# Moving the load buffers of a streaming matrix-vector kernel to a multiple of 4096 bytes in SBUF

## The chip, the cores and the metric

The kernel runs on one core of a Trainium2 chip. The metric is the device time of one execution in microseconds (us), as a median of several.

## The reference, cut to what matters

```python
def setup_inputs():
    B, S, D = 8, 2048, 4096
    # x: (B, S, D) float32, 268 MB;  w: (D, 1) float32

def reference(x, w):
    proj = (x @ w).squeeze(-1)
    cm = np.maximum.accumulate(proj, axis=1)
    is_record = (proj >= cm).astype(np.float32)
    return np.cumsum(is_record, axis=1).astype(np.float32)
```

Every number of `x` is used once. What costs is to bring 268 MB into the core.

## The kernel before

Three buffers of 64 KB in each of the 128 partitions are filled in turn. VectorE (DVE) multiplies the first 2816 columns of every row by `w` and adds them up; GpSimd (POOL) multiplies the other 1280, and ScalarE (ACT) adds those up. The names matter here because the tiles of a pool lie in SBUF in the order in which they are made:

```python
    W2, W2C = 1248, 544
    # ... cut ...
    identity = sb([P, P], "identity")
    small = sb([P, 352], "small")
    masked = sb([P, 2 * P], "masked")
    fold = sb([P, 2 * B - H + Q], "fold")
    w2 = sb([P, W2C], "w2")
    xall = sb([P, NS * R * D], "xall")
    xbuf = [xall[:, i * R * D : (i + 1) * R * D] for i in range(NS)]
    w_sb = sb([P, PC], "w_sb")
    cm = sb([B, N], "cm")
    cnt = sb([B, N], "cnt")
```

The loads of the main part, and the two engines' work on a load:

```python
        for g in range(NG):          # RS = (4, 4, 4, 3) rows for each partition
            r = RS[g]
            for t in range(B):
                i = SY.dma_start(
                    out=at(g, t)[:, : r * D],
                    in_=x[B - 1 - t, STARTS[g] : STARTS[g] + r * P, :].rearrange(
                        "(p r) d -> p (r d)", r=r
                    ),
                ).then_inc(xs[t], 16)
                u, n = user_before(g, t)
                if n:
                    i._wait_ge(*(free(u, n)))     # the buffer's last use
    # ... cut ...
                    i = dot(xb[:, j * D : j * D + VC], w_v[:, :VC], ...)      # DVE
    # ... cut ...
                    i = G.tensor_mul(out=xl, in0=xl, in1=w_sb).then_inc(pl, 1)  # POOL
```

So a packet of a load is the whole run of one partition: 65536 bytes in 24 loads, 49152 in eight. The last 128 rows of each sequence come as 16384-byte rows (six loads), and the last two of those tiles in seven pieces by columns, so that little work is left when the last byte lands:

```python
    LAST = [
        (B - 2, 1696, D, (1696, VC), (VC, D)),      # columns; DVE's; POOL's
        (B - 2, 0, 1696, (0, 1696), None),
        (B - 1, 2592, D, (2592, CV), (CV, D)),
        (B - 1, 1440, 2592, (1792, 2592), (1440, 1792)),
        (B - 1, 736, 1440, (736, 1248), (1248, 1440)),
        (B - 1, 352, 736, (352, 736), None),
        (B - 1, 0, 352, (0, 352), None),
    ]
```

`w2` holds the weights that POOL needs for two of these pieces.

## Time and profile before

| | before |
|---|---|
| median time | 631.98 us (three runs, 631.68 to 632.14) |
| profiled span | 630.0 us |
| bytes read | 268.45 MB |
| address of the load buffers in a partition | 21952 = 85 x 256 + 192 |

From the page of the kernel before: the span, the busy time of each engine, then the share of time in which the DMA engines were busy and what they moved, in 40 equal slices of the span, then the packets.

```profile
span 630.0 us, 1182 instructions
...
PE 31.7 (5%) x108; PEld 15.1 (2%) x108; DVE 406.9 (65%) x292; ACT 180.4 (29%) x273; POOL 370.1 (59%) x147
...
DMA  9999999999999999999999999999999999999995
GB/s 400 399 466 399 466 408 458 421 442 433 433 441 424 445 424 441 425 445 420 449 416 454 412 458 408 458 408 458 408 425 437 444 418 437 444 415 440 416 424 230
DMA packets 6579, 268.55 MB, mean 426 GB/s; under 512 B 768, under 2 KB 1040, under 8 KB 1584
```

The DMA engines are at 90% or more in every slice but the last, while the busiest engine, DVE, works 65% of the span. The GB/s of single slices swing and are not to be read one by one; means over longer stretches are steadier. From the view of stages of before (start and end in us, length, busy time of the engines, granted clock, DMA share, GB/s), a stretch of one load, one of the middle, and one of the 49152-byte packets:

```profile
23.00:42.30 19.30, 0.00 (x0) 0.00 (x0) 12.12 (x8) 5.45 (x8) 11.50 (x4) 1.00 1.00 435
160.00:460.00 300.00, 7.14 (x32) 4.08 (x32) 197.60 (x133) 85.87 (x126) 182.01 (x64) 0.79 1.00 434
460.00:580.00 120.00, 3.29 (x16) 1.94 (x16) 81.01 (x55) 32.81 (x49) 70.42 (x26) 0.51 1.00 432
```

In the stretch of one load (19.3 us) DVE has 12.1 us of work and POOL 11.5, so both wait for the next load. The waits of before (engine and tile that waited, for whom, us in total, times, longest):

```profile
POOL xall L287 <- POOLq L290: 250.2, 32, 20.9
DVE xall L127 <- DMA xall<-in_x_dram: 187.8, 32, 7.9
```

DVE waits for each of the 32 big loads; POOL is started by DVE's signal, so its 250.2 us are the same waits at second hand. The chain of waits of before, in order of time (start, us, what), says so too:

```profile
22.98 0.03 POOLq L290
...
333.61 0.03 POOLq L290
...
345.14 7.81 issue
352.95 0.03 POOLq L290
352.99 11.50 POOL xall L287 x4
364.48 7.83 issue
```

The chain goes through POOL, but every 11.5 us of it is followed by 7.8 us of "issue", time in which POOL waits for something that the view does not name: the landing of the next load, passed on by DVE. What repeats every 19.34 us (352.95 - 333.61) is the load. At the end of the kernel, from the timeline of before (start, us, engine, line, operation):

```profile
623.09 0.99 DVE L127 CUSTOM_DVE_ANT_0 xall<-xall,w_v 128x800 f32<-128x800 f32 x1 [0.26 <-DMA xall<-in_x_dram]
...
624.00 0.68 DVE L127 CUSTOM_DVE_ANT_0 xall<-xall,w_v 128x512 f32<-128x512 f32 x1
...
624.61 0.55 DVE L127 CUSTOM_DVE_ANT_0 xall<-xall,w_v 128x384 f32<-128x384 f32 x1
...
625.09 0.52 DVE L127 CUSTOM_DVE_ANT_0 xall<-xall,w_v 128x352 f32<-128x352 f32 x1
...
627.11 0.34 DVE L149 TENSOR_TENSOR_SCAN cnt_l<-ps,cnt_l,small 8x64 f32<-8x64 f32 x1
```

From 623.09 us on DVE waits for no load any more: its last four pieces run back to back, and a short chain of DVE and two matmuls ends the kernel. One of the four pieces is the one that the change makes wider.

### The profile page before, as it was taken

The numbers are of one execution on the slowest core, as the hardware profiler recorded it, in microseconds if no ns is written. First come the engines' busy times: TensorE is split into PE (matmuls) and PEld (weight loads), VectorE is DVE, ScalarE is ACT, GpSimd is POOL, SyncE is SP. The second block draws the span as 40 slices with busy tenths as digits, with TensorE's granted clock in tenths as the row PEclk, the third lists the DMA queues.
The fourth block names the chain that finished last, engine by engine and source line by source line (L and its number), as shares of the span: only waits on it lengthen the run. The fifth ranks groups of instructions, "written<-read, shape, count | busy, mean of one in ns | idle before, by whom it ended". The sixth has DMA issues, their size and how long they took to land.

```text
span 630.0 us, 1182 instructions
## 1 busy us (share of the span) xinstructions
PE 31.7 (5%) x108; PEld 15.1 (2%) x108; DVE 406.9 (65%) x292; ACT 180.4 (29%) x273; POOL 370.1 (59%) x147
## 2 busy tenths in 40 slices
PE   8000000000010000000010000000002000000031
PEld 3000000000010000000010000000001000000010
DVE  0755676546785557755579555676557966655897
ACT  1222332123322233222233222332223232232353
POOL 0555676446765557755567555576555766666685
PEclk9999999999999999999996555555555555555555
DMA  9999999999999999999999999999999999999995
GB/s 400 399 466 399 466 408 458 421 442 433 433 441 424 445 424 441 425 445 420 449 416 454 412 458 408 458 408 458 408 425 437 444 418 437 444 415 440 416 424 230
DMA packets 6579, 268.55 MB, mean 426 GB/s; under 512 B 768, under 2 KB 1040, under 8 KB 1584
## 3 DMA queue, kind: packets, MB, share of 16 engines
q1 hardware_dynamic: 6560, 268.50, 98.8%
q10 hardware_dynamic: 16, 0.02, 0.0%
q14 instruction: 3, 0.02, 0.0%
HBM read 268.45 MB, written 0.07 MB: 426 GB/s over the span
## 4 chain that ended last, share of the span: by engine, by line
POOL 52%; issue 38%; DMA 6%; PE 2%; DVE 1%; SPq 0%; POOLq 0%; ACT 0%; ACTq 0%
POOL xall L287 52%; DMA xall<-in_x_dram 6%; PE w_v L231 2%; PE ps L231 0%; DVE xall L127 0%; SPq L199 0%; DMA w<-in_w_dram 0%; POOLq L290 0%; ACT w L242 0%; PE ps L373 0%; DVE cm_l L143 0%; DVE cnt_l L149 0%; DVE ps L146 0%; ACT xall L133 0%; DVE masked L365 0%
## 5 line engine op out<-in xcount | busy, mean ns | idle before, releaser
L127 DVE CUSTOM_DVE_ANT_0 xall<-xall,w_v 128x2816 f32<-128x2816 f32 (+3 forms) x133 | 388.4, 2974 | 187.8 <-DMA xall<-in_x_dram 187.8
L287 POOL TENSOR_TENSOR xall<-xall,w_sb 128x1280 f32<-128x1280 f32 x120 | 344.9, 2909 | 250.2 <-POOLq L290 250.2
L133 ACT ACTIVATE xall<-xall 128x1280 f32<-128x1280 f32 (+1 forms) x130 | 162.8, 1252 | 429.7 <-POOL xall L287 417.1
L319 PE MATMUL ps<-identity,small 128*8 128x128 f32 x60 | 13.1, 410 | 572.0 <-PEq L316 572.0
L133 ACT ACTIVATION_READ_ACCUMULATOR xall<-xall 128x1 f32 x130 | 24.2, 186 | 0.0
L343 POOL TENSOR_TENSOR xall<-xall,w_sb 128x1280 f32<-128x1280 f32 (+1 forms) x8 | 21.6, 2704 | 2.8 <-DMA xall<-in_x_dram 2.8
L319 PEld LDWEIGHTS ps<-identity,small 128*8 128x8 f32 x60 | 7.5, 128 | 578.8 <-issue 574.8
L143 DVE TENSOR_TENSOR_SCAN cm<-ps,cm,small 8x512 f32<-8x512 f32 (+1 forms) x5 | 6.1, 1216 | 14.1 <-PE ps L319 14.1
L231 PE MATMUL w_v<-w,identity 8*128 8x512 f32 x14 | 12.1, 1056 | 0.0
L127 DVE DVE_READ_ACCUMULATOR2_ANT small<- 128x1 f32 x133 | 10.8, 82 | 0.0
L253 DVE MEMSET ps<- 8x512 f32 x1 | 0.5, 485 | 15.5 <-ACT w L242 15.5
L149 DVE TENSOR_TENSOR_SCAN cnt<-ps,cnt,small 8x512 f32<-8x512 f32 (+1 forms) x5 | 6.1, 1217 | 0.2
L373 PE MATMUL ps<-fold,masked 128*8 128x64 f32 x32 | 4.6, 303 | 20.1 <-ACT masked L361 13.2
L231 PEld LDWEIGHTS w_v<-w,identity 8*128 8x128 f32 x14 | 4.6, 332 | 7.3 <-issue 7.3
L239 ACT COPY w_sb<-w_v 128x768 f32<-128x768 f32 x1 | 0.8, 799 | 11.4 <-PE w_v L231 11.4
L146 DVE TENSOR_TENSOR ps<-ps,cm 8x512 f32<-8x512 f32 (+1 forms) x5 | 3.3, 660 | 0.2
L373 PEld LDWEIGHTS ps<-fold,masked 128*8 128x8 f32 x32 | 2.5, 112 | 22.4 <-ACT masked L361 14.6
L361 ACT ACTIVATE masked<-fold,small 128x8 f32<-128x8 f32 x9 | 2.5, 297 | 0.2
L231 PE MATMUL ps<-w,identity 8*128 8x512 f32 x2 | 2.1, 1136 | 2.6 <-DMA w<-in_w_dram 2.6
L238 ACT ACT_TABLE_LOAD x1 | 1.3, 1283 | 2.7 <-DVE fold L249 2.7
L245 DVE TENSOR_REDUCE fold<-identity 128x2 f32<-128x128 f32 x1 | 0.3, 286 | 2.1 <-POOL cnt L224 2.1
L343 POOL TENSOR_TENSOR xall<-xall,w 128x352 f32<-128x352 f32 (+1 forms) x2 | 1.5, 766 | 0.2 <-DMA xall<-in_x_dram 0.2
(23 smaller groups left out, 7.0 us busy)
## 6 DMA issues: line engine op xcount, KB each, us to landing
xall<-in_x_dram SPq DMA_DIRECT2D x8, 6144.0 KB, 30.5
xall<-in_x_dram SPq DMA_DIRECT2D x6, 2048.0 KB, 39.5
xall<-in_x_dram SPq DMA_DIRECT2D x1, 1200.0 KB, 33.5
xall<-in_x_dram SPq DMA_DIRECT2D x1, 848.0 KB, 35.1
xall<-in_x_dram SPq DMA_DIRECT2D x1, 752.0 KB, 36.3
xall<-in_x_dram SPq DMA_DIRECT2D x1, 576.0 KB, 37.1
xall<-in_x_dram SPq DMA_DIRECT2D x24, 45.0
xall<-in_x_dram SPq DMA_DIRECT2D x1, 352.0 KB, 17.4
```

What stands on the lines that cost most here:

```text
L127: return V.tensor_tensor_reduce(out=xsl, in0=xsl, in1=wsl, scale=1.0, scalar=0.0, op0=ALU.mult, op1=ALU.add, accum_out=dst,)
L133: return A.activation(out=xsl, in_=xsl, func=ACTF.Copy, accum_out=dst)
L143: V.tensor_tensor_scan(out=cm_, data0=src, data1=low, initial=cm0, op0=ALU.max, op1=ALU.max,)._wait_ge(psr, base).then_inc(psr, 1)
L146: V.tensor_tensor(out=src, in0=src, in1=cm_, op=ALU.is_ge)._wait_ge(psr, base + 1).then_inc(psr, 1)
L149: V.tensor_tensor_scan(out=cnt_, data0=src, data1=low, initial=cnt0, op0=ALU.add, op1=ALU.max,)._wait_ge(psr, base + 2).then_inc(cs, 1)
L231: i = T.matmul(out=dst, lhsT=identity[:NW, k : k + 1].to_broadcast([NW, P]), rhs=w_row, start=True, stop=True,).then_inc(bw, 1)
L238: A.copy(out=w_sb[:, CV - VC :], in_=ps)._wait_ge(bw, 1).then_inc(wc, 1)
L287: i = G.tensor_mul(out=xl, in0=xl, in1=w_sb).then_inc(pl, 1)
L319: i = T.matmul(out=ps[:B, j : r * P : r], lhsT=l[:, j * B : (j + 1) * B], rhs=identity, start=k == 0, stop=k == 1,)
L343: G.tensor_mul(out=xl, in0=xl, in1=w_pool(*p))._wait_ge(xq[i], 16).then_inc(pl, 1)
L361: A.activation(out=e, in_=on, func=ACTF.Copy, scale=acc)._wait_ge(*wait).then_inc(ms, 1)
L373: return T.matmul(out=ps[:B, q : q + Q], lhsT=e, rhs=by_i, start=start, stop=bool(stop),)._wait_ge(*((mg, on_g) if pool else (ms, on_a)))
```

## The change

The intent is to let every load be written to an aligned place. Two small tables move behind the buffers. To make the rest in front of them end on a multiple of 4096, the weights' table `w2` shrinks from 544 to 512 columns (`WC` is 512), and for that one POOL piece gives 32 columns to DVE. No instruction is added or removed.

```diff
-        (B - 1, 736, 1440, (736, 1248), (1248, 1440)),
+        (B - 1, 736, 1440, (736, 1280), (1280, 1440)),
...
-    W2, W2C = 1248, 544
+    W2, W2C = 1280, WC
...
     identity = sb([P, P], "identity")
     small = sb([P, 352], "small")
-    masked = sb([P, 2 * P], "masked")
-    fold = sb([P, 2 * B - H + Q], "fold")
     w2 = sb([P, W2C], "w2")
     xall = sb([P, NS * R * D], "xall")
     xbuf = [xall[:, i * R * D : (i + 1) * R * D] for i in range(NS)]
     w_sb = sb([P, PC], "w_sb")
     cm = sb([B, N], "cm")
     cnt = sb([B, N], "cnt")
+    masked = sb([P, 2 * P], "masked")
+    fold = sb([P, 2 * B - H + Q], "fold")
```

In the built program the buffers' address goes from 21952 to 20480. Each of the three is 65536 bytes long, so all of them have the same remainder.

## The prediction

> **What bounds the kernel now.** The load stream. The slices of the page show the DMA engines at 90% or more in every slice but the last, 426 GB/s over the span; DVE is busy 65%, POOL 59%. In the view of stages, the stretch 23.0 to 42.3 us has DMA share 1.00 at 435 GB/s, with DVE busy 12.1 us and POOL 11.5 us of 19.3. In the view of waits the vector engine waits for loads 187.8 us in 32 waits, one per big load. The chain of waits names POOL for 52%, but every 11.5 us of POOL there is followed by 7.8 us of "issue": it waits for the next load, handed on by DVE. Loads are issued early (median 30 to 45 us to landing, while one load takes 19.3), so the queue never runs dry and a sooner buffer is worth nothing.
>
> **What one load costs.** The trace records each DMA packet. The usual durations are 2418 ns for 65536 bytes, 1815 for 49152 and 611 for 16384. That is a straight line: 27.2 GB/s per engine (435.2 for 16) and about 8.5 ns for each packet. The Trainium skill (DMA: Bandwidth & Descriptors, "Where 436 GB/s comes from") gives the same 435.2 GB/s as the ceiling of the SBUF ports, so this trace agrees. Bytes therefore go at the ceiling already, misaligned or not. Only the constant can shrink: each engine takes 360 data packets, so all of it is about 3 us (estimate: 360 x 8.5 ns).
>
> **What the change does.** The address of the load buffers goes from 21952 (64-byte aligned, 192 past a multiple of 256) to 20480 (a multiple of 4096). The same page ("How a descriptor splits into AXI transactions") lets a start off a 256-byte boundary cost extra beats, a few ns per descriptor; it describes reads, and here reads of full rows start aligned. The trace speaks against even that: the last pieces start 128 bytes past a boundary in HBM and 64 past one in SBUF, and still lie on the same line (9600 bytes: 361 ns, 4608: 178). An 8192-byte instruction fetch took 307 ns, a constant of only 6 ns. If aligned writes reach that, the gain is 360 x 2.8 ns, about 1 us (estimate).
>
> Moved work: the DVE piece of 512 columns becomes 544. From 683 ns (512) against 517 (352), a column is 1.04 ns, so +0.03 us, on the critical path, since DVE runs the last four pieces back to back from 623.1 us. POOL's 192-column product (601 ns) and ScalarE's sum (362 ns) shrink, off the path. The copy of the weights (617 ns for 544 columns) shrinks by about 0.03 us at 17.4 us, before the first load lands at 23: nothing. The moved tables are only touched by small instructions. No instruction is added or removed.
>
> **Prediction.** 631.5 us, range 630.0 to 632.4: essentially the same, with a lean to a gain of some tenths of a us. Faster by over 2%: 0.01; within 2%: 0.98; slower by over 2%: 0.01.
>
> **What would show it.** Right: packets of 65536 bytes at 2415 to 2418 ns; loads landing every 19.3 to 19.4 us as now; the stretch of one load at 432 to 435 GB/s; the tail after the last wait for a load longer by 0.03 us. A gain of the constant would show as 2 to 9 ns less per packet of every size.
>
> **What would make it wrong.** A cost of misalignment hidden in the gaps between packets or in the spread (the mean of 65536-byte packets is 2425, 7 ns over the usual); stalls in the load stream by address (the longest packet took 3455 ns) that vanish with alignment; or aligned buffers colliding with the engines' reads, which would lengthen the dot products (3083 ns) or POOL's products (2909).

## The result, and the profile after

| | before | after |
|---|---|---|
| median, same rounds | 631.85 us (4 runs) | 630.45 us (4 runs, 630.10 to 630.63) |
| ratio | | 0.9977, 95% interval 0.9959 to 0.9994 |
| the same again, on other rounds | 631.68 us (9 runs) | 630.16 us (5 runs), 0.9978, 0.9965 to 0.9992 |
| profiled span | 630.0 us | 628.8 us |

A ratio is the mean time of one kernel's runs over that of the other's of the same rounds, so it is not quite the ratio of the medians. Executions over 1.5% slower than the fastest of the same kernel are left out of the means. The page of the kernel after:

```profile
span 628.8 us, 1182 instructions
...
PE 31.7 (5%) x108; PEld 15.0 (2%) x108; DVE 406.9 (65%) x292; ACT 180.4 (29%) x273; POOL 369.9 (59%) x147
...
DMA  9999999999999999999999999999999999999996
GB/s 401 400 467 400 467 400 467 401 463 404 463 404 463 404 463 404 464 404 463 404 463 404 463 404 467 400 464 404 467 417 444 407 450 441 411 450 441 405 424 248
DMA packets 6579, 268.55 MB, mean 427 GB/s; under 512 B 768, under 2 KB 1040, under 8 KB 1584
```

The engines are as busy as before: DVE 406.9 us, POOL 369.9 against 370.1. The packets are the same in number. The view of stages of after, the same stretches:

```profile
23.00:42.30 19.30, 0.00 (x0) 0.00 (x0) 12.12 (x8) 5.45 (x8) 11.48 (x4) 1.00 1.00 435
160.00:460.00 300.00, 6.78 (x32) 3.88 (x32) 198.20 (x133) 85.88 (x126) 182.56 (x64) 0.53 1.00 435
460.00:580.00 120.00, 3.57 (x16) 1.97 (x16) 80.19 (x55) 33.84 (x49) 70.67 (x26) 0.51 1.00 434
```

The longer stretches read 1 and 2 GB/s higher, which is the direction looked for but no proof: sixteen packets of 65536 bytes more or less in a stretch of 120 us are 9 GB/s, and from 340 to 460 us the same view has 434 before and 432 after. The time from load to load is sharper. The waits of after:

```profile
POOL xall L287 <- POOLq L290: 249.4, 32, 21.0
DVE xall L127 <- DMA xall<-in_x_dram: 186.4, 32, 7.6
```

The chain of waits of after, in order of time:

```profile
23.09 0.03 POOLq L290
...
333.06 0.03 POOLq L290
...
344.57 7.80 issue
352.38 0.03 POOLq L290
352.41 11.49 POOL xall L287 x4
363.90 7.79 issue
```

The timeline of after at the end of the kernel, DVE alone:

```profile
621.75 0.99 DVE L127 CUSTOM_DVE_ANT_0 xall<-xall,w_v 128x800 f32<-128x800 f32 x1 [0.23 <-DMA xall<-in_x_dram]
...
622.75 0.72 DVE L127 CUSTOM_DVE_ANT_0 xall<-xall,w_v 128x544 f32<-128x544 f32 x1
...
623.39 0.55 DVE L127 CUSTOM_DVE_ANT_0 xall<-xall,w_v 128x384 f32<-128x384 f32 x1
...
623.87 0.52 DVE L127 CUSTOM_DVE_ANT_0 xall<-xall,w_v 128x352 f32<-128x352 f32 x1
...
625.89 0.34 DVE L149 TENSOR_TENSOR_SCAN cnt_l<-ps,cnt_l,small 8x64 f32<-8x64 f32 x1
```

From one load to the next it is now 19.32 us (352.38 - 333.06) where it was 19.34 (352.95 - 333.61); over the six loads from there the means are 19.33 and 19.37. From POOL's start on the first load to the end of DVE's last wait for one, the kernel before takes 600.11 us (22.98 to 623.09) and the kernel after 598.66 (23.09 to 621.75), 1.45 us less. The tail from there to the last sum is longer: 4.14 us (621.75 to 625.89) against 4.02 (623.09 to 627.11). The 1.45 us, less these 0.12 and less the 0.11 by which POOL could start later on the first load, are the 1.2 us by which the spans differ.

### The packets one by one

The means above cannot show where in the stream this lies. The trace also holds start, duration and size of each DMA packet. It does not name the engine, but on each of the 16 a packet starts about 4 ns before the one ahead of it ends, so the 16 sequences can be put together. The tables below give the time from one packet's start to the next one's on the same engine, for two of one size. Packets over 25 ns beyond the median, which come in bursts in every run, are left out. For 65536 bytes, where such bursts are commonest early, the mean is over the quiet stretch from 320 to 460 us. "Over the bytes" subtracts the size at 27.2 GB/s, the slope of the prediction. The durations of before and after, as recorded:

```
size     packets   before: min  median  mean     after: min  median  mean
16384      768            611    613   614.8            611    611   611.0
49152     1024           1815   1818  1819.9           1815   1815  1815.2
65536     3072           2415   2420  2424.9           2415   2418  2424.5
```

The shortest packets are equally long before and after. What changed is the spread: before, most took some ns more than the shortest. Starts tell it more sharply (ns from packet to packet, in brackets over the bytes):

```
size     packets on an engine    before           after            less
16384            48              611.7 (9.4)      607.7 (5.3)      4.0
49152            64              1816.5 (9.4)     1812.4 (5.3)     4.1
65536           192              2418.8 (9.4)     2414.8 (5.4)     4.0
```

It is the same 4 ns for three sizes, where the stream is quiet. Early in the stream it is not there: from 20 to 80 us the packets of 65536 bytes (bursts left out) took 7.9 ns over the bytes before and 7.3 after, and 7.6 in e1, which has the old address, as in e11, which is the changed kernel again. So the first third of the big packets gained little or nothing; why is not known. The 128 big packets of an engine after 160 us and its packets of the two other sizes make 128 x 4.0 + 64 x 4.1 + 48 x 4.0 = 0.97 us. The seven last pieces, from the end of the last 16384-byte packets to the end of the last piece (means of sixteen ends), took 10.77 us before and 10.39 after (10.67 in e1, 10.44 in e11), which is 0.2 to 0.4 us less. The sum, 1.2 to 1.35 us, is an estimate to be held against 1.45 us of the stream in the two profiles and 1.40 us between the medians.

### The profile page after: what moved, and what is told of

It reads as the page before. It is cut to its first block, busy times and chain, and to the rows that moved or that the text cites. A ratio compares the mean times of both kernels' runs of the same rounds, so it can differ in the third digit from the quotient of the medians.

```text
span 628.8 us, 1182 instructions
## 1 busy us (share of the span) xinstructions
PE 31.7 (5%) x108; PEld 15.0 (2%) x108; DVE 406.9 (65%) x292; ACT 180.4 (29%) x273; POOL 369.9 (59%) x147
## 4 chain that ended last, share of the span: by engine, by line
POOL 52%; issue 38%; DMA 6%; PE 2%; DVE 1%; SPq 0%; POOLq 0%; ACT 0%; ACTq 0%
POOL xall L287 52%; DMA xall<-in_x_dram 6%; PE w_v L231 2%; DVE xall L127 0%; PE ps L231 0%; DMA w<-in_w_dram 0%; SPq L199 0%; POOLq L290 0%; ACT w L242 0%; PE ps L373 0%; DVE cm_l L143 0%; DVE cnt_l L149 0%; DVE ps L146 0%; ACT xall L133 0%; DVE masked L365 0%
```

## The experiments

The theory is that the place of the buffers alone makes the gain, by a constant for each packet. The rivals are the 32 columns or the moved tables; the old place as such; and, within the theory, which multiple is needed, whether the cost counts packets or bytes, on which side of the transfer it arises, and whether the start as such is paid for or the block of 256 bytes that it adds. All these kernels gave correct results. Below, "ns" is always the time from packet to packet, as above.

### e1: the change's work at the old address

```diff
 (against the changed kernel)
+    masked = sb([P, 2 * P], "masked")
+    fold = sb([P, 2 * B - H + Q], "fold")
     w2 = sb([P, W2C], "w2")
+    sb([P, 32], "gap")
...
-    masked = sb([P, 2 * P], "masked")
-    fold = sb([P, 2 * B - H + Q], "fold")
```

> The changed program (544-column DVE piece, 160-column POOL piece, 512-column weight copy) with the two tables back in front and a 128-byte gap, so that the load buffers lie at 21952 as before. Theory (the address alone makes the gain): as before, ratio 1.000, about 631.9 us; packets of 16384 bytes start every 612 ns on an engine, of 49152 every 1816.5, as before (after: 607.8 and 1812.5); their durations spread (611 to 625). Rival (the narrower piece or the moved tables make it): ratio 0.998, about 630.4 us.

Measured: 631.66 us against 631.58, ratio 1.0003 (0.9989 to 1.0017); 611.8 ns for 16384 bytes, 1816.4 for 49152. With the address the gain is gone.

### e2: the work of before at the new address

```diff
 (against before)
-    small = sb([P, 352], "small")
     masked = sb([P, 2 * P], "masked")
-    fold = sb([P, 2 * B - H + Q], "fold")
     w2 = sb([P, W2C], "w2")
+    sb([P, 64], "gap")
...
     cnt = sb([B, N], "cnt")
+    fold = sb([P, 2 * B - H + Q], "fold")
+    small = sb([P, 352], "small")
```

> The program of before (512-column DVE piece, 192-column POOL piece, 544-column weight copy) with the load buffers at 20480 by another order of the tables. Theory (the address): ratio 0.998, about 630.4 us, packets of 16384 bytes every 607.8 ns, of 49152 every 1812.5, all of one size equally long; the tail after the last load 0.03 us shorter than in the changed kernel. Rival (the split or the tables): ratio 1.000, packets every 612 and 1816.5.

Measured: 630.41 us against 631.58, ratio 0.998 (0.9966 to 0.9993); 607.7 and 1812.4 ns. The whole gain is there without the 32 columns and with another order of the tables. The two intervals of e1 and e2 overlap a little, so the times alone would leave a doubt; the packets do not. The 0.03 us of the tail cannot be told apart in such times.

### e3 and e4: 192 and 256 bytes further

```diff
 (against the changed kernel; K = 48 in e3, 64 in e4)
-    xall = sb([P, NS * R * D], "xall")
+    xall = sb([P, NS * R * D + K], "xall")[:, K:]
```

> The changed kernel with the load buffers 192 bytes further, 192 past a multiple of 256 as before, but 192 past a multiple of 4096 where before was 1472 past one. If what counts is the place in a 256-byte block: as before, 612 and 1816.5 ns from packet to packet, ratio 1.000. If it is something about the old absolute place: 607.8 and 1812.5, ratio 0.998.

> The changed kernel with the load buffers 256 bytes further: a multiple of 256, of nothing larger. If blocks of 256 bytes count: as the changed kernel, 607.8 and 1812.5 ns from packet to packet, ratio 0.998. If a multiple of 512 or of 4096 is needed, as the change intends: as before, 612 and 1816.5, ratio 1.000.

Measured: e3 631.60 us, ratio 1.0002 (0.9986 to 1.0017), 611.7 and 1816.4 ns; e4 630.44 us, ratio 0.9982 (0.9966 to 0.9997), 607.7 and 1812.4 ns. Another absolute place with the old remainder of 256 is as slow as before, and that with the moved columns and the moved tables of the change in place. A multiple of 256 that is none of 512 is as fast as the multiple of 4096. So the change asks for more than is needed.

### e5 to e8: 64, 128, 32 and 4 bytes further

The edit is that of e3 with K = 16, 32, 8 and 1. A row of 16384 bytes that starts on a multiple of 256 touches 64 blocks of 256 bytes; from any other start it touches 65.

> The changed kernel with the load buffers 64 bytes past a multiple of 256. Counting theory (a full row then touches 65 blocks of 256 bytes where 64 do, and each block more costs about 4 ns): as before, 612 and 1816.5 ns from packet to packet, ratio 1.000. Short-first-block theory (only a first stretch as short as 64 bytes costs; here the first is 192 bytes): at most half of it, 608 to 610, ratio 0.998 to 0.999.

> Load buffers 128 past a multiple of 256. Counting theory: 612 and 1816.5 ns, ratio 1.000. Short-first-block theory, and what the last pieces of the changed kernel already show (they start 128 past and are as fast as any): 607.8 and 1812.5, ratio 0.998.

> Load buffers 32 past a multiple of 256, not on a multiple of 64. Counting theory: 612 and 1816.5 ns, ratio 1.000. Short-first-block theory (first stretch 224 bytes): 607.8 and 1812.5, ratio 0.998. If writes want multiples of 64 bytes: more than 612, in the worst case half the rate.

> Load buffers 4 bytes past a multiple of 256, the least that a float allows. If only the constant of a packet is touched: 608 to 614 ns for 16384 bytes, ratio 0.998 to 1.001. If a stream that is not on 32-byte lines is slower for each byte: durations of 65536-byte packets well over 2425 ns, ratio over 1.02.

```
        bytes past 256    16384 bytes        49152             65536            median us   ratio to before
e5            64          611.7 (9.4)     1816.5 (9.4)     2418.9 (9.5)         631.64        1.0000
e6           128          611.7 (9.4)     1816.3 (9.2)     2418.3 (8.9)         631.38        0.9998
e7            32          612.8 (10.4)    1817.5 (10.4)    2419.8 (10.4)        632.23        1.0011
e8             4          614.0 (11.6)    1818.6 (11.6)    2421.0 (11.6)        632.36        1.0010
```

The short-first-block theory falls: 64 and 128 bytes past a boundary cost the same 4 ns as 192, where it had asked for at most half and for nothing. The counting theory holds for these three. It does not name the further 1.1 ns of a start that is no multiple of 64, nor the further 2.3 ns of one that is no multiple of 32; why these are there is not known. Nothing is paid by the byte: at 4 bytes the excess is 11.6 ns for 16384 bytes and for 65536. The profiled run of e5 had more of the disturbances than others (span 630.7 us), and its times were as before's all the same.

### e9 and e10: sixteen times as many packets

Each big load is cut into four by columns, so a packet is 4096 bytes. e10 has the buffers 192 bytes further.

```diff
 (against the changed kernel; CUT = 1024; e10 with the edit of e3 as well)
+                for c in range(0, D, CUT):
+                    i = SY.dma_start(
+                        out=at(g, t)[:, : r * D].rearrange(
+                            "p (r d) -> p r d", r=r
+                        )[:, :, c : c + CUT],
...
-                    V.wait_ge(xs[t], 16).then_inc(go, 1)
+                    V.wait_ge(xs[t], 16 * D // CUT).then_inc(go, 1)
```

> The changed kernel (aligned) with each big load cut into four by columns, so that its packets are 4096 bytes: 3944 data packets for an engine where 360 were, the same bytes to the same places. If the constant of an aligned packet (5.3 ns over bytes at 27.2 GB/s) holds for this size too: 3584 x 5.3 ns = 19 us more than the changed kernel, about 649.5 us (ratio 1.028 to before); 156 ns from packet to packet. If small packets cost nothing when they follow one another: 631.

> The same with the load buffers 192 bytes past a multiple of 256. If misalignment costs about 4.1 ns for each packet: 3944 x 4.1 = 16 us over the aligned one, about 666 us (ratio 1.054 to before); 160 ns from packet to packet. If it costs by the byte, or once a load: 1 to 2 us over the aligned one, about 651.

Measured: e9 650.86 us, ratio 1.03 (1.0284 to 1.0315), 155.5 ns from packet to packet (4.9 over the bytes); e10 666.49 us, ratio 1.0551 (1.0535 to 1.0567), 159.9 ns (9.3). The misaligned one is 15.6 us slower for the same bytes in the same number of packets, where 16 were expected of 3944 packets of 4.1 ns. The cost is thus one for each packet. Of the 20.7 us that e9 is over the aligned kernel of the same rounds (630.16, e11), 3584 more packets of 4.9 ns make 17.6; the other 3 us were not traced. The slices of the page of e9 (GB/s):

```profile
GB/s 309 421 421 421 421 421 421 420 421 421 420 422 420 418 422 422 421 422 421 422 421 420 420 422 422 421 421 421 422 421 422 420 421 422 421 421 421 434 431 211
```

The stage of e9 from 340 to 460 us, with the columns as above:

```profile
340.00:460.00 120.00, 2.78 (x14) 1.52 (x11) 75.84 (x51) 32.71 (x48) 68.97 (x24) 1.00 1.02 421
```

The slices of e10:

```profile
GB/s 308 410 410 410 410 410 409 410 409 410 410 410 410 410 410 410 410 409 410 410 409 410 409 409 410 408 411 410 410 410 409 409 410 410 410 410 409 432 425 255
```

The same stage of e10:

```profile
340.00:460.00 120.00, 3.27 (x16) 2.01 (x16) 73.11 (x50) 31.37 (x47) 66.11 (x24) 0.51 1.03 409
```

Both have their DMA engines busy all the time (overlapping packets give a share over 1), at 421 and at 409 GB/s: the share of busy DMA cannot tell a good stream from a poor one.

### e11: the changed kernel again

No edit.

> The changed kernel as it is, beside the same runs of before. If the first comparison stands: ratio 0.9975 to 0.9985, 1.0 to 1.5 us less than before.

Measured: 630.16 us against 631.68, ratio 0.9978 (0.9965 to 0.9992). The first comparison stands.

### e12: which side's start counts

```diff
 (against e9)
+    BOUNDS = (
+        (0, 1056, 2080, 3104, D),
+        (0, 960, 1920, 2880, D),
+        (0, 1184, 2080, 2976, D),
+    )
+    OFF = (0, 0, 32)
...
-    xbuf = [xall[:, i * R * D : (i + 1) * R * D] for i in range(NS)]
+    xbuf = [xall[:, i * R * D + OFF[i] : (i + 1) * R * D + OFF[i]] for i in range(NS)]
...
-                for c in range(0, D, CUT):
+                bounds = BOUNDS[(t if g < NL else t + NS - 1) % NS]
+                for c, c_end in zip(bounds, bounds[1:]):
```

> Which side's start counts, and whether it is the difference between the two. The cut loads with uneven cuts, a set for each of the three buffers, the third buffer 128 bytes further. Packets of 3840 bytes start on a multiple of 256 in HBM and in SBUF (control); those of 4096 bytes 128 past one on both sides; those of 3584 bytes 128 past one in HBM and on one in SBUF. Time from packet to packet over the bytes at 27.2 GB/s: control 4.9 ns in every theory. If blocks touched in SBUF count: 4096 about 9.3 (17 blocks for 16), 3584 about 4.9. If the difference of the two starts counts: 4096 about 4.9, 3584 about 9.3. If blocks on either side count: both about 9.3.

Measured, ns over the bytes by the place of a packet in an unbroken run of its size on one engine (those of 30 ns and more left out):

```
size    start in HBM, in SBUF    packets 1-10   11-20   21-30   31 and on
3840         0, 0                    4.8          4.8     4.9     4.9
4096       128, 128                  4.9          5.9     8.0     9.1
3584       128, 0                    4.8          4.7     4.9     4.9
```

The place in SBUF counts: 128 bytes past a boundary in HBM alone costs nothing, and the same remainder on both sides does not help. That refutes the difference of the two starts and blocks counted on either side. The second line holds more than was asked for. The cost does not show at once: the first ten packets of a misaligned run are as quick as aligned ones, and the full 4 ns are there only after some thirty. Something between the two sides of the transfer seems to take up a shortfall of some tens of ns first; what it is was not tested.

These packets and the full rows are all whole numbers of 256-byte blocks long, so they do not tell a misaligned start from the block more that it touches. Another size of the same trace does. Packets of 4736 bytes start 128 bytes past a boundary in SBUF too, but end on one: 19 blocks, as many as from a boundary. In their unbroken runs of 32 they stay at 4.8, 4.7 and 4.8 ns over the bytes (packets 1-10, 11-20 and 21-30), where those of 4096 bytes, with the same start and 17 blocks for 16, are at 4.9, 5.9 and 8.0. The last pieces of other runs agree, by the usual duration of a packet:

```
            9600 bytes: blocks (from a boundary)   ns     6784 bytes: blocks (from a boundary)   ns
before              38 (38)                       361             28 (27)                       264
after               38 (38)                       361             27 (27)                       258
e5                  39 (38)                       371             27 (27)                       258
```

So what is paid for is one more 256-byte block in SBUF than the length needs, and not the start alone.

The run took 652.1 us, a single one, beside 631.67 of before.

## Why the prediction was right, and where it was not

- **What bounds the kernel** was right: the load stream does. A change of some ns in each packet moved the end of the kernel, and the engines' work stayed as it was (DVE's product of 2816 columns took 3082 ns before and 3081 after in the mean).
- **"Only the constant can shrink"** was right. Bytes go at the same 27.2 GB/s in every version, and the excess is the same for 16384 and 65536 bytes. The Trainium skill (DMA: Bandwidth & Descriptors, "Where 436 GB/s comes from") gives 435.2 GB/s for the 16; the slope agrees, and an aligned packet of 65536 bytes every 2414.8 ns on 16 engines is 434.2 GB/s.
- **The size of the constant** was off. The prediction took 2.8 ns a packet from one short instruction fetch, about 1 us in all, and then put its central value at only 0.35 to 0.5 us of gain, since "the trace speaks against even that". The term measured 4.0 ns on 304 packets, and the gain was 1.4 us.
- **"The trace speaks against even that"** was the step that failed. It read the usual or shortest duration of packets of two of the last pieces, and found them on one line. Two things were wrong with it. The shortest packet of a size is the same before and after (611 ns); the cost is in the mean and in the time from start to start, which the prediction itself named as what would make it wrong ("hidden in the gaps between packets or in the spread"). And the two pieces were poor witnesses: the one of 9600 bytes touches no more blocks from its misaligned start than from a boundary (38), and the one of 4608 touches 19 for 18 but has a usual duration of 178 ns before and after. The piece of 6784 bytes, with a block more, stood in the same trace at 264 ns, where the line of the prediction gives 258; after the change it takes 258. That 630.45 us still lay within the predicted 630.0 to 632.4 is owed to the width of that range, not to the central value.
- **The guess on the mechanism** was half right. The same page ("How a descriptor splits into AXI transactions") tells of reads that start off a 256-byte boundary. The boundary is 256 bytes here too (e4, e6), but it is the write into SBUF that pays, for a block more (e12); a read 128 bytes past a boundary cost nothing in e12 (4.9 against 4.9 ns). Why one block more costs 4 ns stays open.
- **The tail** was predicted 0.03 us longer and was 0.12. The piece itself is right: 0.61 us from its start to the next before (624.00 to 624.61), 0.64 after (622.75 to 623.39). The other 0.09 us lie ahead of it: 1.00 us after the start of the piece before, where the kernel before has 0.91. Most of it is scatter of single traces: from the start of the 800-column piece to the last sum, the twelve traces with the 544-column piece have 4.05 to 4.14 us, 4.08 in the mean, and the two with 512 columns (before, e2) 4.02 and 4.06. That fits the 0.03 us.
- **The shorter copy, POOL's and ScalarE's shorter pieces, the moved tables** were worth nothing that these times show, as predicted (e1, with the shorter pieces, 1.0003 of before; e3, with the moved tables as well, 1.0002).

## What to carry to other kernels

In a kernel that loads at the ceiling, let each destination run in SBUF start on a multiple of 256 bytes, so that it touches no more 256-byte blocks than its length needs; it costs only an order of the tiles, and more than 256 gained nothing here. The gain is about 4 ns for each packet and engine (in the big packets of the first third of this kernel it did not show), so it is worth asking how many packets there are: 0.2% with 64 KB runs, 2.4% with 4 KB runs (666.49 against 650.86 us). And the number of packets itself costs about as much as their alignment: some 5 ns each, aligned, and the cut kernel was 3% slower than before with its buffers aligned.

## What the Trainium skill lacked or had wrong

- DMA: Bandwidth & Descriptors, "How a descriptor splits into AXI transactions": for a start off a boundary it tells of reads alone. Here a write into SBUF whose run touches one 256-byte block more than its length needs costs 4.0 to 4.1 ns a packet (9.4 against 5.3 ns over the bytes), 5.1 ns when it starts 32 bytes past a boundary and 6.3 when it starts 4 past; a run that starts 128 past and ends on a boundary costs nothing more (4736 bytes: 4.7 to 4.8 ns over the bytes).
- The same section: its extra beats for a read off a 256-byte boundary did not show in HBM loads from packet to packet (4.9 ns for 128 bytes past, 4.9 on the boundary).
- The same page, "Why small descriptors are slow": it gives a fixed overhead of about three cycles a packet, 3.5 ns at the 850 MHz of the page (estimate), as a matter of small descriptors. In these unbroken loads the constant was 4.9 to 5.4 ns aligned and 9.3 to 9.5 misaligned, for 4096 to 65536 bytes alike; 4096-byte packets reached 421 GB/s aligned and 409 misaligned.
- No page tells that such a cost is hidden at first: the first ten misaligned packets after aligned ones ran as if aligned (4.9 ns), the full cost (9.1 ns) came after some thirty.
- SBUF — State Buffer, "Operand start alignment": it says of its rule that it is about legality, not speed. A line on the speed of loads belongs there; the numbers are those above.
